# Unread dense products behind the modulation blocks and in the chain of states of a hybrid encoder

## The chip, the cores and the metric

The kernel runs on one core of one Trainium2 chip. The metric is the device time of one execution in microseconds. Engine names are those of the profile: PE is TensorE's matmul, PEld its weight load, DVE VectorE, ACT ScalarE, POOL GpSimd, SP the queue that issues the DMAs.

## The reference

Two layers of an encoder over 1024 tokens of width 1024, in float32. Each layer is a mixer and an MLP, both with a modulated norm ahead and a gated residual behind. Cut to what matters here:

```python
cond = jax.nn.silu(c)
for l in range(DEPTH):
    mod = cond @ w_mod[l] + b_mod[l]
    sh1, sc1, g1, sh2, sc2, g2 = split(mod, 6)
    h = rms_norm(x) * (1.0 + sc1) + sh1
    z = h @ w_in[l]
    # A: grouped-query attention, B: differential attention,
    # C: gated linear recurrence, forward and backward, by chunks:
    #   new_state = exp(blast) * state + (k * exp(blast - bcum)).T @ v
    x = x + g1 * (concat(o_a, o_b, o_c) @ w_out[l])
    h = rms_norm(x) * (1.0 + sc2) + sh2
    x = x + g2 * (square(relu(h @ w_ff1[l])) @ w_ff2[l])
return rms_norm(x, final_norm)
```

## The kernel before

Activations are kept transposed, with the features on the 128 partitions and two halves of 512 tokens. The large projections split both operands into a rounded part and a rest (hi and lo) and run three products of the rounded type, 128x512 each (`mm3`, lines 291 to 293). Norm sums, the modulation and parts of the recurrence run on plain float32 operands. `cst` holds three 128x128 matrices, among them `ones`.

The order on each engine is written by a scheduler, which places the recorded operations by its own estimate of time and by priorities. The start and part C (the recurrence) have a raised priority. Each engine then works through its list in order.

**The start.** Lines 884 to 889 load x, square it on ACT (line 324), sum over the features on PE with `ones` as the weights (line 326, float32, 128x512; eight for each half of the tokens) and multiply x by the reciprocal root (DVE, line 889, after lines 301 to 306). `modulation_start` then makes shift and scale of the first norm in eight blocks. For each block, eight small products with the block of weights (line 265) give two rows, ACT copies them (line 267), two products with one column each turn them into columns (line 270), into the PSUM tile `pt`, and DVE adds them to `modc` (line 272). Behind each block, h is made for both halves: `h_hi` on ACT (line 897), the unrounded value on DVE (line 898), the rest `h_lo` on POOL or DVE (line 899). The first input projections (lines 291 to 293) take the eight pieces of h as they come. Their PSUM tiles are two buffers with the tag `mm`; `pt` and the tile ahead of it share two buffers with the tag `aux`.

**The chain of states.** `scan_c` first runs seven steps over the chunks for both directions and both pairs of heads (lines 674 to 710). A step sums gate logarithms into `es` (line 687) and `tot` (line 691, two columns each), takes their exponentials on ACT (`ex`, line 694, and `lam`, line 696), multiplies `ex` with the values (`up`, line 700), and updates the states on DVE in eight small operations (line 708), which read `lam` and `up`. `es`, `tot` and `up` take turns in the two `mm` buffers, so the `tot` of a step has to wait for the update before it. The scheduler puts pieces of attention between the steps: scores (line 449), the maximum on DVE (line 455), the exponential on ACT (line 457), transposes (line 473) and products with the values (line 481). The chain runs once in each layer. After it the fronts, scores and outputs of the recurrence (lines 715 to 836) run with the rest of the attention.

Of the kernel before, what the change touches and what calls it, by code (L numbers as in the profile page):

```python
# [19 lines left out]
P = 128  # L20
# [16 lines left out]
NIN = 3  # L37
MB = 3
WAT = 4
LH = 8  # L40
OPRE = (3, 4, 5)
DEFER = (True, False)
# [115 lines left out]
def tile_hybrid_encoder(ctx: ExitStack, tc: tile.TileContext, I, out, depth=DEPTH, dbg=None):  # L158
    nc = tc.nc
# [15 lines left out]
    def mmt():  # L175
        return psmm.tile([P, HALF], F32, name="mm", tag="mm")

    def auxt():
        return psx.tile([P, HALF], F32, name="aux", tag="aux")
# [4 lines left out]
    cst = const.tile([P, 3, P], F32, name="cst")  # L184
    ident, ones, bones = cst[:, 0, :], cst[:, 1, :], cst[:, 2, :]
# [63 lines left out]

    mod_pending = []  # L250

    def modulation_start(l, pool, hook):

        cw = pool.tile([P, KT, 32], F32, name="cw", tag="cw", bufs=1)
        nc.gpsimd.memset(cw, 0.0)
        nc.vector.tensor_copy(cw[:, :, 0:1], cond.unsqueeze(2))
        m2 = modc[l][:, 0:16].rearrange("p (s j) -> p s j", s=2)
        for j in range(KT):
            w = pool.tile([P, KT, 2 * P], F32, name="mw8", tag="mw8", bufs=MB)
            dma(w.rearrange("p k n -> p (k n)"), I["w_modh"][j])  # L260
            hook(j)
            ps = auxt()
            for kt in range(KT):
                q = 32 * (kt % 4)
                nc.tensor.matmul(ps[q:q + 32, 0:2 * P], cw[:, kt, :], w[:, kt, :], start=kt < 4, stop=kt >= 4)
            rows = pool.tile([P, 2 * P], F32, name="mrow", tag="mrow", bufs=2)
            nc.scalar.copy(rows, ps[:, 0:2 * P])
            pt = auxt()
            for i in range(2):
                nc.tensor.matmul(pt[:, i:i + 1], rows[:, i * P:(i + 1) * P], ones[:, 0:1], start=True, stop=True)  # L270
            m = m2[:, :, j:j + 1]
            nc.vector.tensor_add(m, m, pt[:, 0:2].unsqueeze(2))
            yield j
# [4 lines left out]
    def wunit(pool, src):  # L278
        if isinstance(pool, list):
            pool.append(pool.pop(0))  # L280
            pool = pool[-1]
        raw = pool.tile([P, D], F32, name="w_raw", tag="w_raw", bufs=raw_bufs[0])
        dma(raw, src)
        hi = pool.tile([P, D], F32R, name="w_hi", tag="w_hi")
        nc.scalar.copy(hi, raw)  # L285
        lo = pool.tile([P, D], F32R, name="w_lo", tag="w_lo")
        nc.gpsimd.tensor_sub(lo, raw, hi.bitcast(F32))  # L287
        return hi, lo
# [47 lines left out]
    def norm_out(hpool):  # L336
        return [hpool.tile([P, KT, HALF], F32R, name=n, tag="h") for n in ("h_hi", "h_lo")]
# [309 lines left out]
    def scan_c(cf, cp, l, hgain, fronts_done):  # L647
# [26 lines left out]
        for i in range(NCH - 1):  # L674
            ch = (i, NCH - 1 - i)
            lf = cf.tile([P, 2, 2, 4, P], F32R, name="lf1", tag="lf2")
            vv = cp.tile([P, 2, 2, P], F32, name="vv1", tag="vp2")
            for d in range(2):
                for pr in range(2):
                    dma(lf.bitcast(F32)[:, d, pr, :, :], s.lf[pr][ch[d], :, d, :, :])  # L680
                dma(vv[:, d, :, :], s.cv[ch[d]].rearrange("p (a b) -> p a b", a=2))
            es = mmt()
            tot = mmt()
            for d in range(2):
                o = es[:, d * 256:(d + 1) * 256]
                for k in range(4):
                    nc.tensor.matmul(o, sct[:, d, :] if k < 2 else idr, lf[:, d, :, k, :], start=k == 0, stop=k == 3)
            for d in range(2):
                for pr in range(2):
                    for hl in range(2):  # L690
                        nc.tensor.matmul(tot[:, (2 * d + pr) * 2:(2 * d + pr) * 2 + 2], lf[:, d, pr, hl, :], onr,
                                         start=hl == 0, stop=hl == 1)
            ex = cf.tile([P, 2, 2, P], F32, name="ex1", tag="ex1", bufs=2)
            nc.scalar.activation(ex.rearrange("p a b c -> p (a b c)"), es, AF.Exp)
            lam = cf.tile([P, 8], F32, name="lam1", tag="lam1")
            nc.scalar.activation(lam, tot[:, 0:8], AF.Exp)
            up = mmt()
            for d in range(2):
                for pr in range(2):
                    nc.tensor.matmul(up[:, (2 * d + pr) * P:(2 * d + pr + 1) * P], ex[:, d, pr, :], vv[:, d, pr, :],  # L700
                                     start=True, stop=True)
            for d in range(2):
                nx = ch[d] + 1 if d == 0 else ch[d] - 1
                for pr in range(2):
                    for b in range(2):
                        bs = slice(64 * b, 64 * b + 64)
                        u = up[bs, (2 * d + pr) * P + 64 * b:(2 * d + pr) * P + 64 * b + 64]
                        nc.vector.scalar_tensor_tensor(
                            st[bs, d, pr, nx, bs], st[bs, d, pr, ch[d], bs], lam[bs, (2 * d + pr) * 2:(2 * d + pr) * 2 + 1],
                            u, op0=ALU.mult, op1=ALU.add)  # L710
# [168 lines left out]
    def hook(j):  # L879
        if j == WAT:  # L880
            ready.extend(wunit(first_in[1]["w"], I["w_feat"][0, t]) for t in (T_BK, T_BQ))
# [20 lines left out]
    for l in range(depth):  # L902
# [241 lines left out]
        def ffn_half(xh, h, groups, wide, finish=None):  # L1144
            groups = list(groups)
            if not groups:
                return
            prev = ff1(h, w1_units(groups[0]))
            for k, g in enumerate(groups):
                nxt = ff1(h, w1_units(groups[k + 1])) if k + 1 < len(groups) else None  # L1150
                w2 = w2_units(g)
                if finish is None or nxt is not None:
                    ff2(xh, w2, prev, wide)
                else:
                    for c0 in range(0, HALF, TAILW):
                        ff2(xh, w2, prev, wide, c0, TAILW)
                        finish(slice(c0, c0 + TAILW))
                prev = nxt

        def ffn_both(xa, ha, xb, hb, groups, hook):  # L1160
# [19 lines left out]
            if not last:  # L1180
                nxt.append(norm_out(h_["h"]))
            ffn_half(xb, hb, range(LH), True, lambda cs: tail(1, xb, cs, tiles))

        nxt = []

        def tail(half, xh, cs=slice(0, HALF), tiles=None):
            ts = slice(half * HALF + cs.start, half * HALF + cs.stop)
            if dbg is not None and l == 0:
                for j in range(KT):
                    dma(dbg["x2"][j * P:(j + 1) * P, ts], xh[j][:, cs])  # L1190
            if not last:
                for j in range(KT):
                    dma(scr[l + 1].x[j][half][:, cs], xh[j][:, cs])
            y = norm_stats(npool, xh, auxt, "ffr", half in (FINPE if last else ONPE), cs, tiles)
            if not last:
                dst = nxt[half] if half < len(nxt) else None
                r = norm_apply(npool, h_["h"], xh, y, l + 1, 0, half not in NIP, LOPOOL[half], cs, dst)
                if dst is None:
                    nxt.append(r)
                return  # L1200
            for j in range(KT):
                x = xh[j][:, cs]
                if j % 3 == 2:
                    nc.scalar.activation(x, x, AF.Copy, scale=fing[:, j:j + 1])
                    nc.gpsimd.tensor_mul(x, x, y)
                else:
                    nc.vector.scalar_tensor_tensor(x, x, fing[:, j:j + 1], y, op0=ALU.mult, op1=ALU.mult)
                dma(out[j * P:(j + 1) * P, ts], x)

        def hook(g):  # L1210
            modulation_sums()
            if l + 1 < depth and 0 <= g - LH < 6:
                modulation(l + 1, mpool, (2 * (g - LH), 2 * (g - LH) + 1), False)

        x0, h0 = out_proj(0, f_["x"], o_["h"], heads0, [j for j in range(KT) if j not in OPRE])
        ffn_half(x0, h0, range(LH - 1), False)
        actx.close()
# [3 lines left out]
        x1, h1 = out_proj(1, x_["x"], h_["h"], None, range(KT))  # L1221
        ffn_half(x0, h0, range(LH - 1, LH), True)
        ffn_both(x0, h0, x1, h1, range(LH, NG), hook)
        hT = nxt
# [62 lines left out]
```

## Time and profile before

| | |
|---|---|
| median of 3 runs | 3313.77 us (3310.73 to 3320.69) |
| profiled execution, its own time | 3307.72 us |
| its span, first to last instruction | 3305.9 us |
| mean granted TensorE clock | 0.97 of full speed |
| busy: PE, DVE, ACT, POOL | 95%, 59%, 45%, 41% |

The profile has one execution. Its time is 1.8 us more than its span and 6.05 us less than the median. A float32 product stands in the trace as two records; busy times of records overlap by the drain of a product, so the distance from start to start tells what one costs in a row. Granted clock 1.00 is 2.4 GHz and 0.50 is 1.2 GHz; values between are means over a stretch.

### The profile page before, as it was taken

How to read it: one execution, taken by the hardware profiler on the slowest of the kernel's cores; microseconds unless marked ns; L12 is line 12 of the kernel's file. 1: busy time of each engine (PE TensorE's matmuls, PEld its weight loads, DVE VectorE, ACT ScalarE, POOL GpSimd, SP SyncE). 2: the span in 40 equal slices, each digit the busy share in tenths (PEclk: the TensorE clock that was granted, in tenths of full speed). 3: DMA queues.
4: the chain of work that ended last, by engine and by line, in shares of the span. 5: the costliest groups of instructions: out<-in, count | busy, mean ns of one | idle time of the engine just before them, and what ended most of it. 6: DMA issues, size and time to landing. Idle time of an engine off the chain costs nothing.

```text
span 3305.9 us, 44801 instructions
## 1 busy us (share of the span) xinstructions
PE 3153.7 (95%) x16604; PEld 2544.8 (77%) x16604; DVE 1962.9 (59%) x2641; ACT 1476.5 (45%) x2847; POOL 1353.2 (41%) x875
## 2 busy tenths in 40 slices
PE   7999889999899999999999999899999999999998
PEld 4887667777677888887878867777777778888886
DVE  6577865557764555546463776665678545333545
ACT  4345665566652312213333566566667423211322
POOL 3444412324455433324545553132344443333453
PEclk8999989999999999999999999899999999999999
DMA  6566364435425244413234543834342421111222
GB/s 237 174 201 196 121 207 148 121 88 161 124 82 174 79 133 135 136 56 108 96 108 136 179 126 110 244 110 130 106 145 93 156 94 57 52 51 51 83 96 77
DMA packets 214458, 411.79 MB, mean 125 GB/s; under 512 B 35929, under 2 KB 92377, under 8 KB 213217
## 3 DMA queue, kind: packets, MB, share of 16 engines
q1 hardware_dynamic: 214240, 408.93, 39.2%
q8 instruction: 132, 2.16, 0.3%
q14 instruction: 86, 0.70, 0.1%
HBM read 335.43 MB, written 73.40 MB: 124 GB/s over the span
## 4 chain that ended last, share of the span: by engine, by line
PE 69%; DVE 11%; DMA 7%; ACT 5%; issue 4%; POOL 2%; SPq 1%; DVEq 0%; ACTq 0%; POOLq 0%
PE mm L291 11%; PE mm L292 11%; PE mm L293 11%; PE S L291 5%; PE S L292 5%; PE S L293 5%; PE aux L481 4%; PE aux L473 4%; PE S L449 4%; PE mm L779 2%; DMA mw<-in_w_mod 2%; DVE col L455 2%; PE mm L744 1%; ACT pr L457 1%; DVE macc L232 1%
## 5 line engine op out<-in xcount | busy, mean ns | idle before, releaser
L287 POOL TENSOR_TENSOR w_lo<-w_raw,w_hi 128x1024 fp32r<-128x1024 f32 x272 | 667.9, 2463 | 636.0 <-ACT w_hi L285 613.6
L291 PE MATMUL mm<-h_hi,w_hi 128*128 128x512 f32 x1472 | 594.6, 405 | 10.0 <-ACT z L435 4.0
L292 PE MATMUL mm<-h_lo,w_hi 128*128 128x512 f32 x1472 | 586.0, 398 | 6.3 <-POOL h_lo L899 4.1
L293 PE MATMUL mm<-h_hi,w_lo 128*128 128x512 f32 x1472 | 582.7, 397 | 1.8 <-POOL w_lo L287 1.7
L285 ACT CAST w_hi<-w_raw 128x1024 fp32r<-128x1024 f32 x272 | 281.4, 1048 | 603.5 <-PE S L292 244.5
L455 DVE TENSOR_REDUCE col<-S 128x1 f32<-128x1024 f32 x288 | 349.9, 1225 | 125.8 <-PE S L449 124.3
L1141 DVE SCALAR_TENSOR_TENSOR x<-S,modc,x 128x512 f32<-128x512 f32 (+1 forms) x416 | 283.4, 724 | 226.4 <-PE S L293 226.3
L457 ACT ACTIVATE pr<-S,col 128x1024 f32<-128x1024 f32 x288 | 323.5, 1124 | 129.1 <-DVE col L455 69.8
L1118 DVE TENSOR_TENSOR ff_r<-ff_r 128x512 f32<-128x512 f32 x128 | 186.3, 1458 | 321.3 <-ACT act L1117 321.2
L291 PEld LDWEIGHTS mm<-h_hi,w_hi 128*128 128x128 f32 x1472 | 280.9, 191 | 82.4 <-issue 5.9
L292 PEld LDWEIGHTS mm<-h_lo,w_hi 128*128 128x128 f32 x1472 | 281.1, 191 | 74.7 <-issue 5.6
L293 PEld LDWEIGHTS mm<-h_hi,w_lo 128*128 128x128 f32 x1472 | 281.0, 191 | 66.3 <-POOL w_lo L287 2.8
L1119 POOL TENSOR_TENSOR act<-ff_r,act 128x512 fp32r<-128x512 f32 x128 | 168.6, 1318 | 395.3 <-DVE ff_r L1118 390.0
L291 PE MATMUL S<-act,w_hi 128*128 128x512 f32 (+1 forms) x832 | 318.9, 384 | 2.8 <-DVE x L1141 2.5
L292 PE MATMUL S<-act,w_hi 128*128 128x512 f32 (+1 forms) x832 | 317.8, 382 | 1.5 <-POOL act L1119 1.5
L293 PE MATMUL S<-act,w_lo 128*128 128x512 f32 (+1 forms) x832 | 315.3, 383 | 0.4 <-POOL w_lo L287 0.4
L449 PE MATMUL S<-ks,qs 128*128 128x512 f32 x768 | 245.9, 428 | 26.2 <-ACT pr L457 12.6
L1116 ACT ACTIVATE ff_r<-mm 128x512 f32<-128x512 f32 x128 | 76.1, 595 | 407.2 <-PE mm L293 404.0
L473 PE MATMUL aux<-cst,pr 128*128 128x128 f32 x1536 | 231.4, 287 | 20.4 <-ACT pt L474 7.6
L473 PEld LDWEIGHTS aux<-cst,pr 128*128 128x128 f32 x1536 | 187.4, 147 | 65.5 <-issue 14.6
L401 PE MATMUL mm<-w_hi,h_hi 128*128 128x256 f32 x640 | 185.1, 290 | 16.3 <-ACT z L624 13.3
L481 PE MATMUL aux<-pt,vt 128*64 128x256 f32 x1536 | 198.9, 388 | 1.2 <-ACT pt L474 1.2
(232 smaller groups left out, 5821.7 us busy)
## 6 DMA issues: line engine op xcount, KB each, us to landing
w_raw<-in_w_ff SPq DMA_DIRECT2D x192, 512.0 KB, 3.3
mw<-in_w_mod SPq DMA_DIRECT2D x160, 256.0 KB, 2.9
ks<-bk SPq DMA_DIRECT2D x192, 128.0 KB, 3.2
lf<-g_st SPq DMA_DIRECT2D x64, 256.0 KB, 3.4
oT<-o SPq DMA_DIRECT2D x64, 256.0 KB, 4.9
lf<-lf SPq DMA_DIRECT2D x16, 1024.0 KB, 6.6
w_raw<-in_w_out SPq DMA_DIRECT2D x32, 512.0 KB, 3.3
w_raw<-in_w_feat SPq DMA_DIRECT2D x28, 512.0 KB, 4.0
```

The costliest lines, as they stand in the source:

```text
L285: nc.scalar.copy(hi, raw)
L287: nc.gpsimd.tensor_sub(lo, raw, hi.bitcast(F32))
L291: nc.tensor.matmul(ps, wh, ah, start=first, stop=False)
L292: nc.tensor.matmul(ps, wh, al, start=False, stop=False)
L293: nc.tensor.matmul(ps, wl, ah, start=False, stop=last)
L449: nc.tensor.matmul(sp[:, hh * HALF:(hh + 1) * HALF], q[:, sl], ks[:, hh * HALF:(hh + 1) * HALF], start=i == 0, stop=i == len(qs) - 1)
L455: nc.vector.tensor_reduce(nm, sp, axis=AX.X, op=ALU.max, negate=True)
L457: nc.scalar.activation(p, sp, AF.Exp, bias=nm, accum_out=z)
L473: nc.tensor.transpose(tp[:, j * P:(j + 1) * P], p[:, kt * P:(kt + 1) * P], ident)
L481: nc.tensor.matmul(ps[64 * c:64 * c + 64, 0:256], vt[:, kt, :], pts[c][kt // 4][:, kt % 4, :], start=kt == 0, stop=kt == KT - 1)
L1118: nc.vector.tensor_mul(r, r, r)
L1141: nc.vector.scalar_tensor_tensor(x, sp[:, k * HALF:k * HALF + n], g2[:, j - 1 + k:j + k], x, op0=ALU.mult, op1=ALU.add)
```

## The change

A helper `dense` is added that multiplies `ones` with all three matrices of `cst` (128x384, float32) into columns 128 to 511 of a PSUM tile that is there already. It is called with a count of two in two places: on `pt` of each of the eight modulation blocks, and on `tot` of each of the seven steps of the chain, in both layers. Nobody reads these columns. They are 16 and 28 products, 44 together.

```diff
@@ -37,6 +37,8 @@
 WAT = 4
+FILLM = 2
+FILLC = 2
 LH = 8
@@ -249,6 +251,11 @@
     mod_pending = []
+    def dense(bank, n):
+
+        for _ in range(n):
+            nc.tensor.matmul(bank[:, P:4 * P], ones, cst.rearrange("p i n -> p (i n)"), start=True, stop=True)
+
     def modulation_start(l, pool, hook):
@@ -268,6 +275,7 @@
             for i in range(2):
                 nc.tensor.matmul(pt[:, i:i + 1], rows[:, i * P:(i + 1) * P], ones[:, 0:1], start=True, stop=True)
+            dense(pt, FILLM)
             m = m2[:, :, j:j + 1]
             nc.vector.tensor_add(m, m, pt[:, 0:2].unsqueeze(2))
@@ -690,6 +698,7 @@
                         nc.tensor.matmul(tot[:, (2 * d + pr) * 2:(2 * d + pr) * 2 + 2], lf[:, d, pr, hl, :], onr,
                                          start=hl == 0, stop=hl == 1)
+            dense(tot, FILLC)
             ex = cf.tile([P, 2, 2, P], F32, name="ex1", tag="ex1", bufs=2)
             nc.scalar.activation(ex.rearrange("p a b c -> p (a b c)"), es, AF.Exp)
```

In both places the semaphore that the reader of the tile waits for (the addition to `modc` on DVE, the exponential `lam` on ACT) is raised by the second dense product, no longer by the last product whose values are read.

The list of TensorE in the start, from before the last sums of the first norm (`n_sq`; `mw` is a block's weights, `mrow` its rows). Before:

```order
L326 MATMUL mm<-n_sq,cst 128x512 x2
L270 MATMUL aux<-cst,mrow 128x1 x2
L265 MATMUL aux<-mw_374,cw 32x256 x8
L291 MATMUL mm<-h_hi,w_hi 128x512
L326 MATMUL mm<-n_sq,cst 128x512
L292 MATMUL mm<-h_lo,w_hi 128x512
L326 MATMUL mm<-n_sq,cst 128x512
L270 MATMUL aux<-cst,mrow 128x1 x2
```

The same place in the changed kernel, whose lines are numbered up to nine higher (line 334 is line 326 of before, 277 is 270, 272 is 265, 299 is 291, 257 is the dense product):

```order
L334 MATMUL mm<-n_sq,cst 128x512 x2
L299 MATMUL mm<-h_hi,w_hi 128x512
L277 MATMUL aux<-cst,mrow 128x1 x2
L257 MATMUL aux<-cst 128x384 x2
L272 MATMUL aux<-mw_378,cw 32x256 x7
L334 MATMUL mm<-n_sq,cst 128x512
L272 MATMUL aux<-mw_378,cw 32x256
L334 MATMUL mm<-n_sq,cst 128x512
```

The pair of the second block stands ahead of the last two sums of the norm; the pair of the first block stands ahead of four of them. The other six pairs come behind the norm, each right behind its block's columns.

The list of TensorE in the third step of the chain of layer 0 (`lf_4565` is its gate logarithms). Before:

```order
L449 MATMUL S<-ks,qs 128x512 x2
L687 MATMUL mm<-lf_4565,sct 128x256 x2
L687 MATMUL mm<-lf_4565,sck 128x256 x2
L687 MATMUL mm<-lf_4565,sct 128x256 x2
L687 MATMUL mm<-lf_4565,sck 128x256 x2
L691 MATMUL mm<-onr,lf_4565 128x2 x8
L700 MATMUL mm<-vv_4566,ex_4591 128x128 x4
L473 MATMUL aux<-cst,pr 128x128 x8
```

The same step in the changed kernel (457 is line 449 of before, 695 is 687, 699 is 691, 709 is 700, 481 is 473):

```order
L457 MATMUL S<-ks,qs 128x512 x4
L695 MATMUL mm<-lf_4585,sct 128x256 x2
L695 MATMUL mm<-lf_4585,sck 128x256 x2
L695 MATMUL mm<-lf_4585,sct 128x256 x2
L695 MATMUL mm<-lf_4585,sck 128x256 x2
L699 MATMUL mm<-onr,lf_4585 128x2 x8
L257 MATMUL mm<-cst 128x384 x2
L709 MATMUL mm<-vv_4586,ex_4613 128x128 x4
L481 MATMUL aux<-cst,pr 128x128 x8
```

The pair stands between `tot` and `up` in every step, and more scores stand in a step than before. Behind the chain the lists differ in a few places of layer 0, and in more of layer 1, up to the end of the recurrence.

## Rows read from the trace of the kernel before

**Rows 1.** The page's count of busy time, share of the span and instructions, by engine.

```profile
PE 3153.7 (95%) x16604; PEld 2544.8 (77%) x16604; DVE 1962.9 (59%) x2641; ACT 1476.5 (45%) x2847; POOL 1353.2 (41%) x875
```

**Rows 2.** Busy time by stretch: PE, PEld, DVE, ACT, POOL, granted clock, DMA share, GB/s.

```profile
0.00:40.00 40.00, 28.11 (x119) 12.31 (x119) 14.82 (x30) 20.23 (x35) 6.83 (x9) 0.90 0.94 348
40.00:70.00 30.00, 23.96 (x122) 14.36 (x122) 29.05 (x41) 12.89 (x19) 12.80 (x7) 0.67 0.48 159
70.00:84.00 14.00, 14.00 (x61) 11.33 (x60) 6.04 (x10) 4.58 (x7) 12.20 (x9) 0.89 0.27 99
464.00:510.00 46.00, 43.56 (x285) 34.61 (x285) 32.61 (x73) 23.99 (x50) 3.44 (x4) 0.91 0.95 289
2084.00:2132.00 48.00, 42.54 (x270) 37.17 (x271) 33.54 (x81) 23.86 (x57) 3.79 (x6) 0.86 0.95 283
512.00:780.00 268.00, 261.68 (x1745) 204.60 (x1745) 158.81 (x262) 163.94 (x481) 88.35 (x109) 0.99 0.40 118
2132.00:2400.00 268.00, 266.03 (x1810) 207.66 (x1809) 157.52 (x258) 166.31 (x483) 88.60 (x108) 1.00 0.38 117
```

**Rows 3.** Timeline of TensorE in the start: start us, busy us, line, tiles, shape, records.

```profile
21.42 1.92 PE L326 MATMUL mm<-n_sq,cst 128*128 128x512 f32 x2
23.26 1.94 PE L265 MATMUL aux<-mw,cw 128*32 128x256 f32 x16
...
28.38 1.98 PE L326 MATMUL mm<-n_sq,cst 128*128 128x512 f32 x4
30.20 0.50 PE L270 MATMUL aux<-cst,mrow 128*128 128x1 f32 x4
...
33.92 0.50 PE L270 MATMUL aux<-cst,mrow 128*128 128x1 f32 x4
...
61.47 0.50 PE L270 MATMUL aux<-cst,mrow 128*128 128x1 f32 x4
```

**Rows 4.** Timeline of VectorE in the start, same columns.

```profile
32.97 0.47 DVE L230 TENSOR_SCALAR macc<-mw,cond 128x512 f32<-128x512 f32 x1
...
35.16 0.67 DVE L301 TENSOR_SCALAR n_acc<-mm 128x512 f32<-128x512 f32 x1
...
64.08 0.14 DVE L272 TENSOR_TENSOR modc<-modc,aux 128x2 f32<-128x2 f32 x1
```

**Rows 5.** Timelines of GpSimd and TensorE where the start ends.

```profile
67.37 1.50 POOL L899 TENSOR_TENSOR h_lo<-x,h_hi 128x512 fp32r<-128x512 f32 x1 [2.08 <-DVE x L898]
...
68.92 0.79 PE L292 MATMUL mm<-h_lo,w_hi 128*128 128x512 f32 x1 [1.29 <-POOL h_lo L899]
...
73.05 0.40 PE L293 MATMUL mm<-h_hi,w_lo 128*128 128x512 f32 x1
```

**Rows 6.** Timeline of TensorE in one step of layer 0's chain.

```profile
483.10 1.02 PE L691 MATMUL mm<-onr,lf 128*128 128x2 f32 x8 [1.47 <-DVE st L708]
483.98 1.14 PE L700 MATMUL mm<-vv,ex 128*128 128x128 f32 x8
```

**Rows 7.** Timeline of VectorE beside it: the state updates of two steps.

```profile
480.50 2.46 DVE L708 SCALAR_TENSOR_TENSOR st<-st,lam,mm 64x64 f32<-64x64 f32 x8
...
485.44 2.45 DVE L708 SCALAR_TENSOR_TENSOR st<-st,lam,mm 64x64 f32<-64x64 f32 x8
```

**Rows 8.** Who waited for whom (us in total, times, longest) in both chains.

```profile
PE mm L691 <- DVE st L708: 1.9, 2, 1.5
...
DVE st L708 <- ACT lam L696: 7.6, 3, 5.3
```

**Rows 9.** Busy time by stretch of 4 us in the chains, columns as in rows 2.

```profile
488.00:492.00 4.00, 3.71 (x17) 3.30 (x18) 3.37 (x5) 1.55 (x4) 0.00 (x0) 0.67 1.05 336
492.00:496.00 4.00, 4.00 (x29) 3.67 (x29) 3.22 (x11) 2.17 (x7) 0.00 (x0) 0.90 1.06 311
...
2088.00:2092.00 4.00, 4.00 (x19) 4.00 (x20) 1.71 (x7) 0.58 (x1) 0.72 (x1) 0.50 0.63 161
2124.00:2128.00 4.00, 3.79 (x16) 3.26 (x16) 3.79 (x11) 2.00 (x8) 0.35 (x2) 0.57 1.11 214
```

## The prediction

> **What bounds the kernel now.** I read the page's count of busy time first. The matmul part of TensorE is busy for 95% of the span and no other engine for more than 59% [rows 1], so time given to TensorE is lost unless it falls into a hole or makes other products cheaper. Next I read the stretches that the change touches [rows 2]; the reader should look at three columns in each: TensorE's busy time, VectorE's, and the granted clock.
>
> The start has two stages. Up to about 34 us TensorE sums the squares of the norm between the first blocks. From 40 to 70 us VectorE is the limit: it is busy for 29.05 of 30 us, while TensorE has 6.0 us idle and a mean clock of 0.67 [rows 2]. A mean of 0.67 between the levels 0.50 and 1.00 means that two thirds of the stretch, 19.8 us, were spent at 1.2 GHz. The stage ends when GpSimd writes a last piece of h at 67.37 and the projections take it at 68.92, still at half speed until about 73 [rows 5]. From 70 to 84 TensorE has no idle time [rows 2].
>
> The two chains of states are the stretches from 464 to 510 and from 2084 to 2132. TensorE is idle for 2.4 us in the first and 5.5 us in the second, at clocks of 0.91 and 0.86 [rows 2]. The timelines show how a step hangs together: `tot` (line 691) starts at 483.10 after 1.47 us of idling for the state update, `up` (line 700) follows at 483.98 [rows 6], and the updates of two following steps start at 480.50 and 485.44, 4.9 us apart [rows 7]. In the other direction the update waits for `lam`, 7.6 us in the second chain [rows 8]. So a step is a ring: update, `tot`, `lam` and `up`, update. The attention between the steps fills most of what is left on TensorE and VectorE.
>
> **What one dense product costs.** No float32 product of 384 columns stands in the trace. The nearest are the sums of line 326, also float32 with `ones` as weights, with 512 columns. At full clock two of them (four records) start at 28.38 and the next work at 30.20: 1.82 us, or 0.91 each. At half clock one (two records) runs from 21.42 to 23.26: 1.84 us [rows 3]. Three quarters of that are 0.68 and 1.38 us; a pair costs 1.37 us at full clock and 2.8 at half. If columns saved nothing, a pair would cost 1.82. I take 1.37, since both prices above doubled with the clock as streaming columns do. The 22 pairs are 30.1 us of TensorE.
>
> **The eight pairs of the modulation.** Two pairs stand ahead of the last sums of the norm, where TensorE has no holes: 2.7 us. Before, these sums were done when the next work began at 33.92 [rows 3], but VectorE read them only at 35.16, because it had begun products of the later modulation at 32.97 [rows 4]. That hides 1.2 us, and 1.5 us go on. VectorE, which is the limit from there on, passes them to the end of the stage. The other six pairs, 8.2 us, lie in the stage where TensorE has 6.0 us idle and much half-speed work. The addition to `modc` now waits for its pair, and what VectorE has queued behind it, the values of h, waits too. The last block shows the room: its columns were issued at 61.47 and done about half a microsecond later [rows 3], and VectorE came to the addition at 64.08 [rows 4]. These 2.1 us cover a pair at full clock and all but 0.7 us of one at half. I count the six at nothing; without that cover they would cost up to 8.2 us. Against this stands the clock behind the stage: 0.89 over 14 us is 3.1 us at half speed [rows 2], and with a pair shortly ahead of it I expect that to be at full speed, which returns 1.5 us. The start comes out at 0. Its ends are minus 2.5 us (the 1.5 returned, and the 0.95 us in which VectorE was idle) and plus 11.0 (all eight pairs on the path).
>
> **The fourteen pairs of the chains.** They cost 14 x 1.37 = 19.2 us, and the order puts each between `tot` and `up`. Both ways around the ring pass it: `lam` waits for the second product by its semaphore, `up` stands behind it in TensorE's list. So the pair itself doesn't fill the hole in front of `tot`; it lengthens the step. What it gives back is indirect: while TensorE runs the pair, VectorE does maxima of the attention that would have delayed the update later. The new order has more scores in a step, which fits. Between absorbing nothing and all 7.9 us of idle time I take half, 4.0. Then the clock: within the chains 488 to 496 and 2124 to 2128 have clocks of 0.67, 0.90 and 0.57 [rows 9], which is 2.6 + 0.8 + 3.4 = 6.9 us at half speed. With a pair in each step I expect these at full clock, which returns half, 3.4 us. Chains: 19.2 - 4.0 - 3.4 = 11.8 us. The ends: 19.2, and 0.4 if all idle time is used and all 21.7 us at half speed in both stretches (8.3 and 13.4, from clocks of 0.91 and 0.86 [rows 2]) become full speed, which returns 10.9.
>
> The rows show the clock both ways: from 2088 to 2092 the matmul engine shows as busy for 4.00 of 4.00 us and stays at 0.50 [rows 9], while by the sums of line 326 it rose between 23 and 28 us [rows 3]. The Trainium skill ("TensorE: Matmul & The Clock Gate", section "What's actually happening") says that "the default state is throttled, and activity releases the throttle". Taken for every pair, that rule gives the chain's lower end above; taken from the row of 2088 alone, nothing would return and the chains would cost 15.2 us.
>
> **The order behind the chains.** The scheduler moved attention and recurrence in places up to the end of part C. There TensorE is idle for 6.3 of 268 us in layer 0 and 2.0 of 268 in layer 1 [rows 2]. A better order could gain these 8.3 us at most, a worse one lose a few; I take 0, with 4 us either way.
>
> **The sum.** 0 + 11.8 + 0 on the profiled execution's 3307.72 us is 3319.5. That execution was 6.05 us under the median of the runs, so against the median the forecast is 3325.6 us, 0.36% slower. About 0.3%, 9.9 us, is what a measurement of this kernel can tell from no change.
>
> **Rivals.** *The clock and the holes pay for it (not slower).* If the pairs keep the clock at its upper level throughout both chains and all idle time there is used, the chains cost 0.4 us, and the start gives 2.5 back: 3311.7 us. For it: the low clock stands just where the pairs go. Against it: much of the low stretch in the chains precedes the first pair (2088 to 2092 does), and the ring leaves the hole in front of `tot` where it was. It decides in its favour if over 13 of the 19.2 us come back. To be faster by over 0.3% it needs the better order of 8.3 us on top.
>
> *Every pair of the chains is on the ring and nothing comes back.* Each step then takes 1.37 us more and the holes stay: 19.2 + 1.5 us, 3334.5. If the additions to `modc` also hold VectorE up in all eight blocks, it is 30.2 us, 3344. For it: the list and the semaphore, which leave no way past the pair. Against it: VectorE's load in the chain, part of which moves into the pair's time.
>
> *The products are cheaper than float32.* If a pair took one pass instead of four, 0.34 us, the chains would cost 4.8 us less the same returns, about nothing: 3314. Against it: line 326 has the same types and weights.
>
> **How the numbers follow.** I give the forecast 0.42, the first rival 0.33, the second 0.20, the third 0.05. The forecast lies just above the bound of 3323.7 us, so 0.30 of its chance is slower and 0.12 the same. The first rival has 0.09 faster and 0.24 the same; the second is slower; the third is 0.01 and 0.04. Together: faster 0.10, the same 0.40, slower 0.50. The range runs from 3306 us, into the first rival with part of the order's gain, to 3339 us, beyond the second rival's chain price; the forecast's own range is 3318 to 3333.
>
> **What would show it.** Two records of line 257 about 0.34 us apart at full clock; the start's last piece of h near 68 us as before; state updates about 1 us further apart than 4.9; the clock from 488 to 496 and 2124 to 2128 near 1.00 in their new places, and TensorE's idle time in the chains at half of 7.9 us. The prediction is wrong if the holes in front of `tot` vanish, if the low clock from 40 to 70 us turns out to have been what held VectorE, or if the order behind the chains moves the time by more than the chains do.

## The result, and the profile after

The changed kernel takes 3331.21 us (median of 15 runs, 3325.04 to 3344.56) against 3313.86 us for the kernel before beside it (median of 15 runs): a ratio of 1.0055, with a 95% interval from 1.0044 to 1.0065, or 18 us more. The forecast was 3325.6 us, 0.36% slower. The time lies in the range and the sign is right, but the sum was made of the wrong terms, as the runs show: the number came out by luck.

The page's count of busy time after the change:

```profile
PE 3170.7 (95%) x16692; PEld 2548.1 (76%) x16692; DVE 1971.6 (59%) x2641; ACT 1477.5 (44%) x2847; POOL 1355.0 (41%) x875
```

Against [rows 1] TensorE has 88 more records (44 products of two) and 17 us more busy time; the span grew by 26.4 us in this pair of executions (3305.9 to 3332.3). Busy time by stretch, with the columns of [rows 2]; the last two stretches are the two chains, from the first sum of `es` to the last `up`:

```profile
0.00:40.00 40.00, 30.59 (x116) 12.86 (x120) 13.29 (x28) 19.60 (x34) 5.60 (x8) 0.91 0.93 342
40.00:70.00 30.00, 24.08 (x147) 14.05 (x139) 29.71 (x40) 12.61 (x20) 13.60 (x7) 0.93 0.50 166
70.00:86.00 16.00, 15.78 (x64) 12.55 (x63) 8.34 (x11) 5.15 (x8) 11.40 (x8) 0.91 0.13 50
472.90:530.40 57.50, 50.58 (x303) 39.32 (x303) 32.23 (x72) 23.05 (x47) 2.70 (x3) 0.94 0.75 224
2106.30:2155.50 49.20, 45.72 (x281) 36.73 (x282) 32.07 (x75) 23.29 (x46) 4.18 (x5) 0.93 0.93 268
```

The same two chains in the kernel before:

```profile
469.80:510.80 41.00, 38.56 (x271) 32.39 (x269) 31.35 (x70) 20.16 (x43) 2.21 (x3) 0.96 0.96 288
2082.80:2124.00 41.20, 35.95 (x240) 31.70 (x240) 27.46 (x69) 19.96 (x40) 3.44 (x4) 0.88 0.93 292
```

The chains are 16.5 and 8.0 us longer. In the start the clock from 40 to 70 us rose from 0.67 to 0.93, and the stage is not shorter: VectorE is busy for 29.71 of the 30 us. In the first chain TensorE's idle time grew from 2.4 to 6.9 us, where the prediction had let it shrink. The timeline of TensorE in the first chain shows where:

```profile
495.13 1.54 PE L257 MATMUL mm<-cst 128*128 128x384 f32 x4
496.21 0.92 PE L457 MATMUL S<-ks,qs 128*128 128x512 f32 x2
...
500.26 1.06 PE L481 MATMUL aux<-cst,pr 128*128 128x128 f32 x8
506.44 2.05 PE L457 MATMUL S<-ks,qs 128*128 128x512 f32 x4 [5.11 <-DMA ks<-ak]
508.28 1.70 PE L699 MATMUL mm<-onr,lf 128*128 128x2 f32 x8
509.84 2.91 PE L257 MATMUL mm<-cst 128*128 128x384 f32 x4
```

The scores (line 457) that open the next heads of attention wait 5.11 us for `ks`, the keys of those heads. `tot` (line 699), which could have run, stands behind them in the list. When TensorE goes on it does so at half speed (the pair at 509.84 takes twice the time of the one at 495.13). The list of who waited for whom in this chain shows the wait beside the one that had been predicted, `lam` for the second product of the pair:

```profile
ACT lam L705 <- PE mm L257: 5.1, 3, 2.4
...
PE S L457 <- DMA ks<-ak: 5.1, 1, 5.1
```

SyncE's queue shows what the load of `ks` stood behind:

```profile
495.30 1.75 SPq L688 DMA_DIRECT2D lf<-lf  x4
497.17 1.09 SPq L520 DMA_DIRECT2D ks<-ak  x2
```

In the kernel before, TensorE's and SyncE's rows for the same heads are these:

```profile
479.97 0.71 PE L449 MATMUL S<-ks,qs 128*128 128x512 f32 x2
...
489.32 2.00 PE L449 MATMUL S<-ks,qs 128*128 128x512 f32 x4 [0.26 <-DMA ks<-ak]
```

```profile
481.96 1.09 SPq L512 DMA_DIRECT2D ks<-ak  x2
```

The load has to wait for the last scores that read the old contents of its buffer, and the first scores of the next heads wait for the load. Before, 9.35 us lay between the two groups of scores (479.97 to 489.32), and that was just enough, with 0.26 us of waiting. In the changed kernel's list TensorE would have been ready 5.1 us after the one (496.21 to 501.33) for the other. The second chain of this trace has such a wait of 1.47 us, and a second execution of the changed kernel (a1 below) has waits of 3.71 and 3.41 us in its two chains. (The trace puts the first of these down to ACT's exponential, which ended just before; but the loads of `ks` landed about 0.65 us before these scores began, as they do before the scores that wait for them in the other traces, so I count it to `ks`.)

### The profile page after: what moved, and what is told of

It reads as the page before. It is cut to its first block, busy times and chain, and to the rows that moved or that the text cites. A ratio compares the mean times of both kernels' runs of the same rounds, so it can differ in the third digit from the quotient of the medians.

```text
span 3332.3 us, 44968 instructions
## 1 busy us (share of the span) xinstructions
PE 3170.7 (95%) x16692; PEld 2548.1 (76%) x16692; DVE 1971.6 (59%) x2641; ACT 1477.5 (44%) x2847; POOL 1355.0 (41%) x875
## 4 chain that ended last, share of the span: by engine, by line
PE 70%; DVE 12%; DMA 6%; issue 4%; ACT 4%; POOL 3%; SPq 0%; DVEq 0%; POOLq 0%; ACTq 0%
PE mm L299 11%; PE mm L300 11%; PE mm L301 11%; PE S L299 5%; PE S L300 5%; PE S L301 5%; PE aux L489 4%; PE S L457 4%; PE aux L481 4%; PE mm L788 3%; DMA mw<-in_w_mod 2%; DVE col L463 2%; PE mm L753 1%; DVE macc L234 1%; POOL w_lo L295 1%
```

## The experiments

The scheduler writes a new order whenever its input changes, so an edit of the program tests two things at once. All kernels here therefore keep one of the two orders on every engine, "the old" (of the kernel before) or "the new" (of the changed kernel), and edit the finished list of instructions. They only add, shorten or leave out products that nobody reads, or move loads; everything that is read is computed as before. In the diffs the conditions are written as names. Each ratio is to the kernel before, timed beside it on the same chip (medians 3310.47, 3314.93 and 3314.13 us in the three sessions); microseconds are the ratio's excess times that median.

| run | order | products | ratio, 95% interval | us |
|---|---|---|---|---|
| f1_new_order_thin | new | all, one column wide | 1.0031 (1.0019 to 1.0043) | +10.3 |
| f2_old_order_full | old | all 22 pairs | 1.0032 (1.0020 to 1.0044) | +10.6 |
| f3_new_order_chain | new | chains full, modulation one column | 1.0054 (1.0039 to 1.0069) | +17.9 |
| f4_new_order_mod | new | modulation full, chains one column | 1.0043 (1.0031 to 1.0055) | +14.2 |
| g1_old_order_chain | old | chains alone | 1.0034 (1.0021 to 1.0047) | +11.3 |
| g2_old_order_mod | old | modulation alone | 1.0022 (1.0012 to 1.0033) | +7.3 |
| g4_old_order_ahead | old | chains alone, ahead of `es` | 1.0010 (0.9998 to 1.0021) | +3.3 |
| n0_new_order_none | new | none | 1.0044 (1.0032 to 1.0057) | +14.6 |
| a1_after_again | new | all (the changed kernel) | 1.0057 (1.0042 to 1.0072) | +18.9 |
| k1_none_loads_first | new, two loads earlier | none | 1.0007 (0.9996 to 1.0018) | +2.3 |
| k3_after_loads_first | new, two loads earlier | all | 1.0021 (1.0008 to 1.0033) | +7.0 |
| o1_old_order_loads_late | old, two loads later | none | 1.0029 (1.0017 to 1.0042) | +9.6 |

A trace holds one execution, and a stage's length in it moves from run to run: the last 900 us, where no edit touches anything, took between 908.3 and 915.6 us in the traces of the old order. The stages are read with that in mind.

### Products and order apart

f1 keeps the new order and cuts every product to one column; f2 keeps the old order and puts the pairs in by hand, ahead of the second column product of a block and ahead of the last two products of `tot`, so that the readers wait for the pair as in the change. f3 and f4 are f1 with one of the two groups left wide.

```diff
 # f1: the finished list of the changed kernel
+    if dense(i):
+        ins[k] = copy.replace(i, outs=[one_column(out)], ins=[one_column(moving), weights])
...
 # f2: the finished list of the kernel before
+    if second_column_product(i) or last_sum_of_tot(i):
+        new += [dense_product(columns 128 to 511 of the same tile)] * 2
     new.append(i)
```

> The changed kernel's lists and semaphores on every engine, word for word, but each of the 44 dense products is cut to one column (128x1) after the lists were written. If the loss is the time of the products (first theory), this is level with the kernel before, 0 +- 3 us, and the chain of layer 0 shrinks from 58.5 us to about 42. If the loss is the new order of the lists (second theory: a wait of 5.1 us for a DMA stands in the chain of layer 0 of the changed kernel and in none of before), this stays 8 to 12 us slower than before. What the product theory and the order theory leave over, a low clock, would show here as it does before: below 1.00 within the chains.

> The lists of the kernel before, unchanged, with the pairs put in by hand: in each modulation block between the two column products, in each step of the chains between the third and the fourth sum of tot, so that the reader waits for the pair as in the change. Product theory: 13 to 20 us slower than before (30.1 us of TensorE, less what holes and clock return). Order theory: 5 to 9 us slower, since the old order keeps its DMAs early.

> The changed kernel's lists; the 28 products of the chains as in the change, the 16 of the modulation cut to one column. By my forecast's terms the modulation costs 0 and this is level with the changed kernel, +17 us on before. From the trace of the change, whose start is 3.3 us longer, it should be 3 us faster than the change: +14 us.

> The changed kernel's lists; the 16 products of the modulation as in the change, the 28 of the chains cut to one column. Product theory: +0 (forecast's term) to +3.3 us (from the trace) on before. Order theory: 8 to 12 us slower than before, like the thin kernel, plus those 0 to 3.3 us. With the run that keeps the chain's products it also tells whether the two places add up.

f2 came out near the product term of the prediction: +10.6 us, between the two ranges that were on record for it. In its trace the start, up to the first product of line 401, lasts 82.9 us (before: 82.8), and the chains 47.5 and 47.2 us (41.0 and 41.3), 12.4 us more. But the new order with products of one column costs as much, +10.3, and the wait for `ks` is in it too (5.2 us before the scores at 499.69). So the order has a price of its own; how much of f1 was the products of one column stayed open, and the next runs took them out. For the modulation's pairs f3 and f4 speak with two voices: f3 is level with the changed kernel (17.9 and 18.2), as the forecast's 0 has it, and not at the +14 expected from the start's length, while f4 is 3.9 us above f1. Neither difference is told from nothing, nor are the two from each other.

### The old order, one group at a time, and the order with no products

```diff
 # g1: f2 without the modulation's pairs; g2: f2 without the chains' pairs
-def insert_dense(nc, count=2, mod=True, chain=True):
+def insert_dense(nc, count=2, mod=False, chain=True):
...
 # g4: g1, each pair ahead of the first sum of es, with that sum's waits
-    c = chain and last_sum_of_tot(i)
+    c = chain and first_sum_of_es(i)
...
 # n0: the finished list of the changed kernel
+    if dense(i):
+        move_semaphore_updates(i, product_before(i))
+        continue
     new.append(i)
```

> The order of the kernel before on every engine, with the 14 pairs of the chains alone put in between tot and up. By the prediction's own term: +11.8 us (0.36%) over the kernel before, 5.9 in each chain, state updates about 1 us further apart, the start and all other stages as before. If every pair lies on the ring and nothing comes back: +19.2 to +20.6 us (14 pairs of 1.37 to 1.47). If clock and holes pay: within 3 us of the kernel before.

> The order of the kernel before, with the eight pairs of the modulation alone. By the prediction: 0, the start as long as the 82.8 us of before (it was 82.9 where all 22 pairs stood in the old order), the clock of the start higher than 0.81. If VectorE's additions to modc wait for the pairs: +8 to +12 us, and the last addition that much later than 64.08. If the higher clock behind the stage pays: up to 2.5 us faster.

> The order of the kernel before, with the 14 pairs of the chains alone, but each put ahead of the sums es that open its step instead of between tot and up, where neither lam nor up wait for it. If the chains are lengthened because the pair stands on the ring from tot to up: clearly cheaper than the same pairs behind tot, +4 to +8 us, since the hole in front of tot can take part of it. If the pairs cost what TensorE's time costs, wherever they stand: the same as behind tot, within 2 us (+9 to +12). If the place ahead of es is worse, because the exponentials wait too: +13 or more.

> The changed kernel's order on every engine, with all 44 products taken out; what waited for the second product of a pair waits for the matmul ahead of it. Theory A, the new order costs by itself: the run with products of one column, +9.9 us, was mostly order, so this one is +7 to +10 us (0.2 to 0.3%), with the wait of some 5 us of the scores for a late load ks and the half-speed stretch behind it still in the first chain, which lasts over 50 us. Theory B, the products of one column were not free: a pair of them takes 0.44 us in that trace (488.87 to 489.31), 22 of them 9.7 us, so without them the new order costs 0 to 2 us, and the first chain is back near 47 us or less.

**The chains' pairs behind `tot`** cost 11.3 us (7.0 to 15.6); the forecast for them was 11.8. **The modulation's pairs** cost 7.3 us alone (4.0 to 10.9), where 0 was forecast; the start shows part of it. In the six traces with no products there it lasts 81.0 to 82.8 us, in the six with full pairs 82.9 to 87.3; the means are 3.0 us apart. The two traces with products of one column there, f1 and f3, lie at 83.9. The two prices do not add up: 11.3 and 7.3 make 18.6, and f2 has both groups of pairs at 10.6 (6.6 to 14.6), on another chip. Why stays open. So the runs put the modulation's price at about 0 to 7 us, and the 3 us of the traces lie in between.

**The place decides.** g4 has the same 14 pairs as g1, 19.2 us of TensorE, and costs 3.3 us (-0.7 to 7.0), a little under the +4 to +8 us on record for it, not told from nothing, and 8 us less than g1; the two intervals only meet at 7.0. The windows over the two chains of g4, and under them those of f2 and of g1, with the same pairs behind `tot`:

```profile
471.00:515.20 44.20, 44.15 (x295) 35.79 (x293) 30.41 (x70) 20.60 (x43) 1.06 (x3) 1.00 0.82 255
2093.30:2135.40 42.10, 39.10 (x266) 32.34 (x264) 26.66 (x65) 18.51 (x39) 3.44 (x4) 0.99 0.89 271
```

```profile
467.40:514.80 47.40, 45.66 (x298) 36.06 (x296) 32.10 (x70) 21.37 (x44) 2.71 (x3) 1.00 0.84 262
2087.30:2134.50 47.20, 43.66 (x268) 35.11 (x269) 28.75 (x71) 20.08 (x40) 3.43 (x4) 0.94 0.83 256
```

```profile
467.50:516.60 49.10, 47.36 (x298) 37.29 (x297) 32.10 (x70) 20.54 (x43) 1.96 (x3) 0.97 0.79 238
2091.70:2143.60 51.90, 46.96 (x268) 37.98 (x269) 29.23 (x71) 20.12 (x40) 3.43 (x4) 0.87 0.79 237
```

Ahead of `es` neither `lam` nor `up` waits for a pair, so TensorE can run it while VectorE updates the states (in g4 the pair from 487.93 runs beside the update from 487.54). In g4's first chain TensorE is idle no more (44.15 of 44.20 us busy), and the clock is full throughout. This is the ring of the prediction seen from the other side: what made the pairs dear was not TensorE's time but standing between `tot` and `up`.

**The new order without a single product costs 14.6 us** (10.6 to 18.9), more than the 7 to 10 us that theory A had on record. Theory B, which had put f1 down to its products of one column, falls. (n0 and f1 are not told apart: their intervals overlap.) TensorE's timeline and the stretches of 4 us show the same stall in n0, and what follows it:

```profile
491.34 0.71 PE L457 MATMUL S<-ks,qs 128*128 128x512 f32 x2
...
496.17 1.06 PE L481 MATMUL aux<-cst,pr 128*128 128x128 f32 x8 [0.26 <-DVE pr L597]
501.50 2.05 PE L457 MATMUL S<-ks,qs 128*128 128x512 f32 x4 [4.26 <-DMA ks<-ak]
```

```profile
498.00:502.00 4.00, 0.51 (x1) 0.50 (x2) 1.49 (x2) 1.21 (x2) 0.00 (x0) 0.85 0.99 212
502.00:506.00 4.00, 4.00 (x17) 3.65 (x16) 2.32 (x4) 1.16 (x3) 0.00 (x0) 0.50 0.58 145
506.00:510.00 4.00, 4.00 (x13) 3.33 (x13) 3.25 (x10) 0.11 (x2) 0.00 (x0) 0.50 0.77 224
```

A stall is paid for twice: 4.26 us of waiting, and then at least 8 us in which TensorE is always busy at half speed. The second chain of n0 has two such waits, 4.39 us for keys of part B (`ks<-bk`) and 5.14 us for those of part A (`ks<-ak`), the loads that the next runs move. Together its chains are 20.8 us longer than those of before (51.6 and 51.5 us).

### The loads of ks

k1 is n0, and k3 the changed kernel, with the first two loads of `ks` in each chain issued ahead of the `lf` loads that stood before them (1 MB each time). o1 is the kernel before with its first two loads of `ks` issued six places later.

```diff
 # k1 and k3, SyncE's list in layer 0 (in layer 1: ahead of one lf load of 1 MB)
+L520 DMA ks<-ak 64x1024 x2
 L688 DMA lf 128x512 x4
-L520 DMA ks<-ak 64x1024 x2
 L532 DMA qs<-aq 64x512
...
 # o1, SyncE's list in layer 0 (in layer 1: behind two vp and four qs)
-L512 DMA ks<-ak 64x1024 x2
 L680 DMA lf 128x512 x2
 L681 DMA vv 128x256
 L680 DMA lf 128x512 x2
 L681 DMA vv 128x256
+L512 DMA ks<-ak 64x1024 x2
 L524 DMA qs<-aq 64x512 x2
```

> The changed kernel once more, on the same chip as the three runs beside it, so that the products can be priced inside its own order: it minus its order without products. The first runs gave 1.0055 for it and 1.0044 for its order alone, which makes the 22 pairs +3.6 us there against +9 to +11 in the old order. If the products are nearly free in the new order (its stalls take them): 1.005 to 1.006 again, and close to the order alone. If the two first batches differed by chip: 1.007 or more.

> The changed kernel's order without products, and in each chain the two loads of ks issued ahead of the lf loads that stood directly before them on SyncE's queue (1 MB each time, about 3 us at the 340 GB/s of that stretch). Theory L (late loads of ks are what the order costs): the waits of 4.3 and 5.1 us of the scores for ks shrink to about 1 to 2 us each, the half-speed stretches behind them too, and the run is 5 to 12 us under the order without products, at +3 to +9 us over the kernel before. Rival Q (the queue is full, something else comes late): the waits move to lf and the time stays at +12 to +15. Rival O (the waits are not on the path): they shrink, and the time stays.

> The changed kernel with all its products and the same two pairs of loads moved ahead of lf. Theory L: 5 to 12 us under the changed kernel, at +6 to +12 us over the kernel before, which is what the products cost in the old order. Rivals Q and O: as the changed kernel, +17.

> The kernel before with no products, and one edit: in each chain the first two loads of ks for the next heads are issued six places later on SyncE's queue, at about 487 instead of 482 and 2125 instead of 2118.5. In the kernel before the first scores on them wait only 0.26 us (at 489.32) and 0.21 us (at 2127.32), so there is no slack to lose. Theory L: waits of 4 to 6 us at both places, half clock behind them, +8 to +15 us in all, near the +14.6 of the new order without products. Rival (a wait there is taken up by the rest of the chain): waits of 4 to 6 us and +0 to +4 us.

Theory L holds in all three, with k1 a little under the +3 to +9 us on record for it. Moving four loads in each kernel brought the new order without products from +14.6 to +2.3 us, and the changed kernel from +18 to +7.0. The same scores in k1, on TensorE's timeline:

```profile
491.74 1.06 PE L481 MATMUL aux<-cst,pr 128*128 128x128 f32 x8 [0.25 <-DVE pr L597]
492.56 1.18 PE L457 MATMUL S<-ks,qs 128*128 128x512 f32 x4
```

And in k3, where the rows from 494.08 to 498.12 are those of the changed kernel from 496.21 to 500.26:

```profile
498.12 1.07 PE L481 MATMUL aux<-cst,pr 128*128 128x128 f32 x8
499.57 1.17 PE L457 MATMUL S<-ks,qs 128*128 128x512 f32 x4 [0.39 <-DMA ks<-ak]
500.58 0.95 PE L699 MATMUL mm<-onr,lf 128*128 128x2 f32 x8
```

The waits of 4.26 and 5.11 us are gone or 0.39 us, and the rows behind are at full speed. In the second chains the wait for `ks<-ak` is gone in both. The other wait of n0's second chain, for `ks<-bk`, was not touched: it is still there in k1, with 4.04 us, and its chains last 46.3 and 44.3 us, 8.4 us more than before. So the +2.3 us (-1.3 to 6.0) still hold a stall in this execution, which is 3.3 us over the median of k1's runs. The chains of k3 last 49.6 and 48.3 us at clocks of 1.00 and 0.93. The view of line 520 gives the time from issue to landing, first in the changed kernel (window 484 to 504), then in k3:

```profile
DMA to landing us min/median/max: 7.9/8.3/8.6
```

```profile
DMA to landing us min/median/max: 3.3/3.5/3.9
```

So the move worked through the queue. The loads were issued about as long after the old scores as before (0.95 us in k3, 0.96 us in the changed kernel); without the 1 MB ahead of them they landed 4.8 us sooner. Over both chains and all six traces of the new order with the 1 MB ahead, these loads took 4.4 to 9.2 us; in k1 and k3 3.3 to 3.9. The Trainium skill ("DMA: Bandwidth & Descriptors", section "Queues, rings and completion order") says that on each DMA engine "descriptors are consumed in ring order"; the landing times agree with that.

o1 shows that the wait is enough by itself: no product, the old order, and +9.6 us. TensorE's timeline and a stretch of 4 us:

```profile
494.62 2.04 PE L449 MATMUL S<-ks,qs 128*128 128x512 f32 x4 [4.51 <-DMA ks<-ak]
```

```profile
494.00:498.00 4.00, 3.38 (x12) 3.02 (x13) 1.22 (x1) 0.00 (x0) 0.00 (x0) 0.50 0.60 173
```

In layer 1 the wait was 3.68 us, before the scores at 2143.55.

## Why the prediction was right in the number and wrong in the terms

**The price of a pair: right.** Four records 0.34 us apart and 1.37 us from the pair to the work behind it: in the changed kernel's second chain the last pair starts at 2154.12 and `up` at 2155.49. The rival of cheaper products is out.

**The start: mis-sized, 0 forecast and about +3 measured in the traces.** Two terms failed: the 1.2 us that were to hide the pairs around the end of the norm, and the 1.5 us that the clock was to return. The cover of the later pairs held. VectorE's additions to `modc` of the first, the fourth and the last block show it, in the kernel before (its last is in [rows 4]) and in g2:

```profile
27.49 0.16 DVE L272 TENSOR_TENSOR modc<-modc,aux 128x2 f32<-128x2 f32 x1 [2.12 <-PE aux L270]
...
40.33 0.15 DVE L272 TENSOR_TENSOR modc<-modc,aux 128x2 f32<-128x2 f32 x1
```

```profile
29.68 0.16 DVE L272 TENSOR_TENSOR modc<-modc,aux 128x2 f32<-128x2 f32 x1 [3.60 <-PE aux L270]
...
44.22 0.16 DVE L272 TENSOR_TENSOR modc<-modc,aux 128x2 f32<-128x2 f32 x1 [0.77 <-PE aux L270]
...
67.97 0.15 DVE L272 TENSOR_TENSOR modc<-modc,aux 128x2 f32<-128x2 f32 x1
```

From the fourth addition to the last it is 23.75 us in both (23.79 in f2), and 18.4 to 18.6 in every trace of the new order, with pairs or without: there the pairs cost nothing. From the first to the fourth it is 12.8 us before, in g1 and in o1 (13.9 in g4), and 14.5 in g2 and f2; in the new order it is 20.9 without products and 22.4 with pairs. So the early pairs cost 1.5 to 1.7 us between these additions. Ahead of the first addition stands one more pair; by the price of a pair it costs up to 1.4 us (an estimate), and together that makes the 3 us. Nothing came back behind the stage: from the last addition to the end of the start it is 18.7 us before and 18.7 and 19.3 in f2 and g2, and the clock from 70 to 86 us is 0.91 in the changed kernel and in the kernel before. That the pairs also raised the clock from 40 to 70 us did not shorten the stage, so the low clock was not what held VectorE. Both the 3 us of the traces and the 7.3 us of g2 lie between the ends of -2.5 and +11.

**The chains: right, for the order that I costed them in.** In the old order the pairs cost 11.3 us against 11.8. By f2's trace the parts are near, too: idle time fell from 7.7 to 5.3 us, 2.4 us absorbed for 4.0 forecast. Half-speed time (the length times twice what the clock lacks of 1) fell from 3.3 + 9.9 to 0 + 5.7 us, which returns half of 7.5 us, 3.8 for 3.4. By g1's trace they are not: its chains are 18.8 us longer than before, with 6.7 us idle and 16.4 us at half speed, so 1.0 us was absorbed and the clock returned nothing, as in the rival "on the ring and nothing comes back". f2's traced execution is 4.7 us under the median of its runs and g1's 4.7 us above. So the total is shown, and the two returned terms are not. In the new order they do not add up like that: the changed kernel is only some 4 us over n0 (18.2 and 18.9 against 14.6), a difference that is not told from nothing; that the stalls of that order take part of the pairs in is my reading. In n0 the chains hold 19.9 us of idle time, in the changed kernel 10.4 and 10.9 in its two traces.

**The order: 0 with 4 us either way, and it was +14.6.** This is the step that failed, twice over. I looked for the order's effect behind the chains, where TensorE had 8.3 us idle, and took that idle time as the bound of a gain, with "a few" for a loss. A loss has no such bound: it is made of waits that the trace of before doesn't show. And the place was inside the chains. The prediction even names the sign of it, "more scores in a step", and reads it as filling; but those scores are the last readers and the first readers of `ks`, and what moved was the distance between them, from 9.35 to 5.1 us, for a load that takes 6.2 to 6.7 us in the first chain of the old order and 7.9 to 8.6 in that of the changed kernel, behind 1 MB of `lf`. The place on the queue counts beside the distance: with the load ahead of `lf`, in k3, the short distance cost 0.39 us.

**The sum.** +11.8 was forecast as products alone, and +18 came, made of +14.6 for the order and some +4 for the products. That it lies in the range is luck: two errors, the order's 14.6 us left out and the products' price too high by some 8 in that order, went against each other. The rival "every pair on the ring and nothing comes back", with 3334.5 us, is nearer to the result than the forecast and is wrong in its reason as well: most of the time is not in pairs. The rival "the clock and the holes pay for it" describes g4, not the change.

**The signs.** Records 0.34 us apart: as forecast (four of them in 1.37 us). State updates about 1 us further apart than 4.9: as forecast where no stall stands between them (479.78, 485.85 and 491.76 in the changed kernel). Last piece of h near 68 us: no, the last addition that it needs ends only after 69.66. Clock near 1.00 in 488 to 496 of the chain: as forecast in f2 (1.00 over the first chain) and less so in g1 (0.97), undone by the stall in the change (0.94). Idle time in the chains halved: in f2 a third, in the change it grew.

**Open.** The last 900 us are shorter in the traces of the new order (905.7 to 907.6 us) than in those of the old (908.3 to 915.6); why wasn't tried. k3's +7.0 and f2's +10.6 are not told apart. Why a pair's place in the list made the scheduler bring the scores closer together wasn't tried either.

## What to carry to other kernels

Where a scheduler writes the order, a change of a few microseconds is two changes. Cost the added work, and then, for every buffer whose load waits on its last reader, compare the distance from the last reader of the old contents to the first reader of the new in both lists with the time that the load takes from issue to landing. A wait of a few tenths of a microsecond on a DMA in the trace of before (here 0.26 and 0.21 us) marks a distance that has no slack. Work that only fills belongs where nothing waits for it: the same 14 pairs cost 11.3 us between `tot` and `up` and 3.3 us ahead of `es`.

## What the hardware showed that I had not expected

The same 256 KB loads from the same queue took 4.4 to 9.2 us from issue to landing with 1 MB issued just ahead of them (8.3 in the first chain of the changed kernel), and 3.3 to 3.9 us without (3.5 in that of k3). A stall of TensorE of 4 to 5 us was followed by a stretch at half speed with TensorE fully busy (0.50 from 508 to 512 us in the changed kernel, and from 502 to 510 in n0). Half of that is lost, at least 2 and 4 us on top of waits of 5.11 and 4.26 us. And filling every hole of the first chain and some of the second, in g4, gave back nearly all that it cost: 19.2 us of products for 3.3 us of time, at clocks of 1.00 and 0.99 where they had been 0.96 and 0.88.
